# Folding the memory's weights outside the mixers of a two-layer hybrid encoder

## Chip, cores, metric

One NeuronCore of a Trainium2 chip runs the whole program; nothing is shared with other cores. The metric is device time of one execution in microseconds, and lower is better.

## What is computed

The trunk has two layers over 1024 tokens of width 1024, in float32. Each layer projects its input into four mixers (axial GQA attention, bidirectional RWKV-7, bidirectional HGRN2, MLA attention), joins them, adds a cross-attention to 256 memory tokens and then a mixture of 32 experts:

```python
for l in range(DEPTH):
    h = x @ w_in[l]
    z_att, z_rwkv, z_hgrn, z_mla = split_sizes(h, (ATT_IN, RWKV_IN, HGRN_IN, MLA_IN))
    ...
    mix = jnp.concatenate([y_att, y_rwkv, y_hgrn, y_mla], axis=-1) @ w_out[l]
    x = layer_norm(DN_ALPHA * x + mix, ln1_g[l], ln1_b[l])
    x = layer_norm(DN_ALPHA * x + memory_cross_attention(x, mem, mem_wq[l], mem_wkv[l], mem_wo[l]),
                   ln2_g[l], ln2_b[l])
    x = layer_norm(DN_ALPHA * x + hierarchical_moe(x, ...), ln3_g[l], ln3_b[l])

def memory_cross_attention(x, mem, wq, wkv, wo):
    q = (x @ wq).reshape(B, S, MEM_HEADS, dh)
    k, v = jnp.split(mem @ wkv, 2, axis=-1)
    ...
    return block_attention(q, k, v, dh ** -0.5) @ wo
```

The memory `mem` is an input of the program, so the products `wq @ k^T` and `v @ wo` of each head don't depend on the tokens. The kernel computes them once per layer ("the fold") and then multiplies the tokens with the folded 1024 x 1024 matrices `wqk` and `vw`.

## The kernel before

Every large product is done in three passes: a float32 operand is split into a high part (ScalarE copies it into the fp32r type) and the remainder (VectorE subtracts), and TensorE multiplies high by high, high by low and low by high into one PSUM bank (`mm3`, L256 to L260). So each weight of 128 x 2048 costs a load of 1 MB, a ScalarE copy and a VectorE subtraction before its last pass can run.

A layer has these stages, in program order (a scheduler then orders each engine's queue from it):

- `in_proj` (L338): eight tiles of 128 tokens come from a generator (`ln_in` for layer 0, the `combine` of the experts' outputs for layer 1). Each is transposed, split and multiplied with the two weights `w_ina` (`values`, 272 columns, L258 to L260), then twenty weights `w_inb` follow (L719). All its raw weights go through the two buffers of the pool `k.raw`.
- The mixers (in `trunk`): `rwkv` runs woven with `beside()`, which first runs the two attentions and then `hgrn` woven with `mem_prep`, the fold. `weave` takes the next step from the generator that is furthest behind its share; the shares are `RW, SPLIT` (rwkv against the rest) and `SHARES` (hgrn against the fold). `SPLIT` 2.13 lets attention, which counts 1, run beside the first 1/2.13 of rwkv's steps.
- `mem_prep` (L1537): per head and layer a product of `mem_wkv` with the memory (twice, for keys and values: 96 matmuls of 256 columns in all), `wqt` with the keys (48 of 256) and the values with `wo` (24 of 512). Over four heads these are 576 matmuls of 256 columns and 96 of 512. Its weights come in pieces of 256 KB through two buffers `mz` (L1549), are split by L1550 (ScalarE) and L1551 (VectorE), and the results are copied out (L1582, L1595) and stored to HBM.
- `Weights` is the ring that loads (L1644) and splits (L1654, L1655) all later weights, up to 10 raw buffers and 4 split ones ahead; `mix_mem` and `moe` take them with `W.next()` and let the next one be split with `W.ahead()`.
- `moe` (L2028): 32 experts; the rows of an expert's output are scattered to HBM (L2078), and `combine` (L2147) loads them again (L2162), adds them (L2178), normalises (L285 to L295) and yields the tiles to the next `in_proj`. Its pools are opened on the right side of the memory, where the ring's buffers were.

## Time and profile before

| what | us |
|---|---|
| median of 3 runs | 3597.49 |
| lowest and highest of them | 3592.26, 3612.54 |
| the profiled execution | 3598.46 |
| its span | 3596.6 |

The profiled execution is 1 us from the median, and 1.9 us of it lie outside its span. In the profile a busy time of an engine is the union of its instructions' spans. Matmuls are pipelined, so that the distance between the starts of two of them is shorter than their duration. A window's row gives the busy time of each engine in a stretch of the span, and the share of full clock that was granted to TensorE there (1.00 is 2.4 GHz, 0.50 is 1.2 GHz).

### The profile page before, as it was taken

To read this page: it belongs to the slowest core of one execution; us is meant where nothing else is said; L and a number is where in the kernel's file an instruction comes from. 1 tells how busy PE (TensorE), PEld (TensorE's weight loads), DVE (VectorE), ACT (ScalarE), POOL (GpSimd) and SP (SyncE) were. 2 spreads that over 40 slices of the span, in tenths; PEclk is the share of its full clock that TensorE was granted. 3 is DMA by queue.
4 is the path that set the end of the run, shared out by engine and by line. 5 is a ranking of instruction groups with operands and counts; after the bars stand their busy time and mean duration, and the time that the engine had idled before them with its cause. 6 is when DMAs were issued, how large, how long until landed. Compare 5 with 4: busy or idle time off the path is not lost. (4 is left out here: it accounts for less than half of the span.)

```text
span 3596.6 us, 57124 instructions
## 1 busy us (share of the span) xinstructions
PE 3179.0 (88%) x22814; PEld 2394.0 (67%) x22814; DVE 2489.7 (69%) x3966; ACT 1577.5 (44%) x2303; POOL 745.1 (21%) x496
## 2 busy tenths in 40 slices
PE   8999799988969997999599888989888699979995
PEld 7867345557857886777487564454677588867772
DVE  6546877668846466899764578767788364669996
ACT  3344333345432222788534353433454323138883
POOL 0000353421020003332210004533200200033323
PEclk9999799899989997999799988988899899979997
DMA  5223411125464132999542252111344741249994
GB/s 212 109 74 134 99 34 46 42 75 152 122 216 157 61 135 108 342 363 372 210 160 109 81 158 43 52 28 45 97 146 119 255 158 59 88 155 362 365 341 186
DMA packets 270217, 545.74 MB, mean 152 GB/s; under 512 B 90608, under 2 KB 170096, under 8 KB 236400
## 3 DMA queue, kind: packets, MB, share of 16 engines
q1 hardware_dynamic: 244496, 486.31, 39.5%
q0 software_dynamic: 24288, 53.52, 4.2%
q8 instruction: 184, 3.01, 0.3%
q10 hardware_dynamic: 1152, 2.10, 0.2%
q14 instruction: 97, 0.79, 0.1%
HBM read 444.29 MB, written 131.07 MB: 160 GB/s over the span
## 5 line engine op out<-in xcount | busy, mean ns | idle before, releaser
L1655 DVE TENSOR_TENSOR wl<-raw,wh 128x2048 fp32r<-128x2048 f32 x202 | 465.2, 2306 | 69.5 <-ACT wh L1654 66.6
L1654 ACT ACTIVATE wh<-raw 128x2048 fp32r<-128x2048 f32 x216 | 413.4, 1914 | 161.8 <-PE y L260 102.4
L1432 POOL TENSOR_TENSOR acc<-acc,pT 128x512 f32<-128x512 f32 x224 | 312.4, 1418 | 326.5 <-PE o L1429 197.0
L258 PE MATMUL bg<-wh,xh 128*128 128x512 f32 x768 | 310.3, 404 | 45.6 <-ACT xh L1696 45.6
L260 PE MATMUL bg<-wh,xl 128*128 128x512 f32 x768 | 307.9, 401 | 5.0 <-DVE xl L1697 4.9
L259 PE MATMUL bg<-wl,xh 128*128 128x512 f32 x768 | 308.2, 401 | 0.0
L1410 DVE TENSOR_REDUCE nm<-c 128x1 f32<-128x512 f32 x236 | 161.8, 685 | 109.8 <-PE c L1409 107.6
L1443 ACT ACTIVATE pT<-b 128x512 f32<-128x512 f32 x224 | 128.1, 595 | 211.2 <-PE b L1441 198.4
L719 PE MATMUL p<-xh,wh 128*128 128x512 f32 x640 | 208.1, 404 | 0.9 <-DVE r L569 0.9
L258 PE MATMUL h<-wh,xh 128*128 128x512 f32 x512 | 207.9, 406 | 0.2 <-ACT xh L309 0.2
L309 ACT ACTIVATE xh<-tp 128x512 fp32r<-128x512 f32 x224 | 122.9, 599 | 185.1 <-PE tp L307 175.7
L260 PE MATMUL h<-wh,xl 128*128 128x512 f32 x512 | 202.5, 395 | 0.0
L259 PE MATMUL h<-wl,xh 128*128 128x512 f32 x512 | 202.3, 395 | 0.0
L719 PE MATMUL p<-xl,wh 128*128 128x512 f32 x640 | 200.3, 392 | 0.0
L719 PE MATMUL p<-xh,wl 128*128 128x512 f32 x640 | 199.4, 391 | 0.0
L258 PEld LDWEIGHTS bg<-wh,xh 128*128 128x128 f32 x768 | 146.6, 191 | 79.1 <-ACT xh L1696 47.2
L1655 POOL TENSOR_TENSOR wl<-raw,wh 128x2048 fp32r<-128x2048 f32 x14 | 63.7, 4565 | 632.3 <-ACT wh L1654 616.9
L958 POOL DMA_DIRECT2D xs<-zlo x48 | 26.5, 556 | 779.3 <-DVE raw L512 660.6
L2078 POOL DMA_INDIRECT ya<-yo,slot x64 | 93.3, 1458 | 403.9 <-DMA ya<-yo,slot 178.1
L260 PEld LDWEIGHTS bg<-wh,xl 128*128 128x128 f32 x768 | 146.2, 190 | 40.3 <-DVE xl L1697 7.9
L259 PEld LDWEIGHTS bg<-wl,xh 128*128 128x128 f32 x768 | 146.6, 191 | 32.1
L310 DVE TENSOR_TENSOR xl<-tp,xh 128x512 fp32r<-128x512 f32 x224 | 146.1, 682 | 29.4 <-ACT xh L309 23.1
(518 smaller groups left out, 8023.5 us busy)
## 6 DMA issues: line engine op xcount, KB each, us to landing
raw<-in_moe_w_dram SPq DMA_DIRECT2D x192, 1024.0 KB
raw<-in_w_inb_dram SPq DMA_DIRECT2D x20, 1024.0 KB
x<-x SPq DMA_DIRECT2D x40, 512.0 KB
mz<-in_mem_wkv_dram SPq DMA_DIRECT2D x64, 256.0 KB
mz<-in_mem_wqt_dram SPq DMA_DIRECT2D x32, 256.0 KB
wqk<-rec SPq DMA_DIRECT2D x32, 256.0 KB
mz<-in_mem_wo_dram SPq DMA_DIRECT2D x32, 256.0 KB
vw<-rec SPq DMA_DIRECT2D x32, 256.0 KB
```

Source lines behind the costliest of these rows:

```text
L258: self.T.matmul(ps, ah, bh, start=start, stop=False)
L259: self.T.matmul(ps, ah, bl, start=False, stop=False)
L260: self.T.matmul(ps, al, bh, start=False, stop=stop)
L309: self.S.activation(out=h, in_=p, func=AF.Copy)
L310: self.V.tensor_tensor(xl[:, 4 * j:4 * j + 4], p, h.bitcast(F32), ALU.subtract)
L719: T.matmul(p[i], a, b[i][:, kk], start=(kk == 0 and a is h and b is xh), stop=(kk == 7 and a is lo))
L1410: V.reduce_max(nm[:, j, t, c:c + 1], b, axis=AX.X)
L1432: G.tensor_tensor(acc[j], acc[j], p[j], ALU.add)
L1443: S.activation(out=p[j], in_=b, func=AF.Exp, scale=scale)
L1654: k.S.activation(out=h, in_=raw, func=AF.Copy)
L1655: (k.G if pool else k.V).tensor_tensor(lo, raw, h.bitcast(F32), ALU.subtract)
L2078: G.indirect_dma_start(out=y_d, out_offset=bass.IndirectOffsetOnAxis(ap=ai, axis=0), in_=y, in_offset=None, bounds_check=2047, oob_is_err= ...
```

## The change

The fold leaves the mixers. `mem_prep` becomes a generator that takes its weights, banks and staging buffers from its caller. Layer 0's runs inside `in_proj`: after each tile's transposes three of its 24 steps are issued, before the `values` of the tile ahead. Layer 1's runs at the end of layer 0's `moe`, behind the last expert's `down`, with its weights supplied by the same `Weights` ring; for this, three buffers of the ring (`W.late`) are lent to the memory tokens from expert 26 on. All weights of the fold now come as whole 1 MB loads. `ln_in` has two buffers where it had three, hgrn has four PSUM banks where it had two, and the shares in the weave are new: attention runs beside the first 1/1.5 of rwkv.

```diff
-RW, SPLIT, ATT, SHARES = 420, 2.13, 1 / 90, (70, 12)
+RW, SPLIT, ATT, HGRN = 420, 1.5, 1 / 90, 1 / 157
...
 def ln_in(k):
-        pl = k.pool(es, "lnin", 3, side="right")
+        pl = k.pool(es, "lnin", 2, side="right")
...
 def in_proj(k, l, src, fold):
+        def folding():
+                load = lambda dt=F32: k.t(k.raw, [128, 2176], "raw", dt)[:, :2048]
+                raw = load().rearrange("p (k n) -> p k n", k=8)
+                nc.sync.dma_start(raw, A["mem_t"])
+                mem = [k.t(pl, [128, 8, 256], t, F32R) for t in ("mh", "ml")]
+                k.split_into(raw, *mem)
...
+                def weight():
+                    raw = load()
+                    nc.sync.dma_start(raw, next(srcs))
+                    h, lo = k.t(pl, [128, 2048], "fh", F32R, bufs=2), load(F32R)
+                    k.split_into(raw, h, lo)
+                    return h, lo
...
         for t, x in src:
             k.transpose_split(x, xh[t // 4][:, :, o:o + 128], xl[t // 4][:, :, o:o + 128], pt)
+            for _ in islice(extra, 3):
+                pass
             if t:
                 values(t - 1)
+        for _ in extra:
+            pass
         values(7)
...
+def mem_prep(k, mem, weight, done, bank, wide, stage, halves, wqk, vw):
...
+    for hd in range(4):
+        kh, kl = mem_proj()
+        yield
+        wh, wl = weight()
+        for g in range(2):
+            b = wide()
...
+            dma(wqk[hd - hd % 2 + g, :, :, n], out(b).rearrange("p (m n) -> p m n", m=4))
             yield
...
+        vh, vl = mem_proj()
+        yield
+        wh, wl = weight()
+        for t in range(2):
+            b = wide()
...
 class Weights:
     def fetch(self, q=None):
+        if self.lent and self.wr[0] is self.late:
+            self.wr.popleft()
+            return
...
 def moe(k, l, x2_d, lg, sl, W, fold):
+            if e == 26 and fold:
+                W.lend()
+        ht, w2 = turn(pt, h), W.next()
+        down(py, ht, w2, aid[:, 31:32])
+        if fold:
+            W.ahead()
...
+            for _ in mem_prep(k, (mh, ml), W.next, W.ahead, lambda: k.t(ps, [128, 512], "h"), wide,
+                              lambda: k.t(pl, [128, 1024], "yo", bufs=NY), spare, *fold):
+                pass
...
 def trunk(nc, tc, A, out, nl=2, dbg=None):
-                        sh = k.pool(es3, "psh", 2, PSUM)
-                        sm = k.pool(es3, "psm", 2, PSUM)
-                        yield from weave([hgrn(k, Z, l, mix_d, cp, ph, sh, pe, first),
-                                          mem_prep(k, l, raw, wqk, vw, ph, pe, sm)], SHARES)
+                        sh = k.pool(es3, "psh", 4, PSUM)
+                        for c in hgrn(k, Z, l, mix_d, cp, ph, sh, pe, first):
+                            yield (c or SMALL) * HGRN
```

SyncE's queue at the program's start, where the first weights are loaded. Before:

```order
L365 DMA raw_159<-in_w_ina_dram 128x2176
L334 DMA xd_71<-y_76 128x1024
L365 DMA raw_165<-in_w_ina_dram 128x2176
L328 DMA x_191<-in_x_dram 128x1024
L328 DMA x_277<-in_x_dram 128x1024
L328 DMA x_363<-in_x_dram 128x1024
L365 DMA raw_869<-in_w_inb_dram 128x2048
L365 DMA raw_991<-in_w_inb_dram 128x2048
```

Now (`mem_t` is the memory, `mem_wkv` and `mem_wqt` are the fold's weights; all go through the two buffers of `k.raw`):

```order
L369 DMA raw_163<-in_w_ina_dram 128x2176
L338 DMA xd_71<-y_76 128x1024
L369 DMA raw_169<-in_w_ina_dram 128x2176
L332 DMA x_329<-in_x_dram 128x1024
L430 DMA raw_198<-in_mem_t_dram 128x2048
L332 DMA x_516<-in_x_dram 128x1024
L437 DMA raw_204<-in_mem_wkv_dram 128x2048
L332 DMA x_727<-in_x_dram 128x1024
L332 DMA x_914<-in_x_dram 128x1024
L437 DMA raw_263<-in_mem_wqt_dram 128x2048
L338 DMA xd_71<-y_331 128x1024
L338 DMA xd_71<-y_518 128x1024
```

The fold's loads follow the two of `w_ina` at once, and those of `w_inb` come behind the fold.

TensorE's queue in the same stage. Before, the values of tile 0 (`p<-w,x`) follow the first transposes:

```order
L307 MATMUL tp_177<-ident,y_76 128x128 x4
L307 MATMUL tp_184<-ident,y_76 128x128 x4
L258 MATMUL p_223<-wh_161,xh_138 128x272
L259 MATMUL p_223<-wl_162,xh_138 128x272
L260 MATMUL p_223<-wh_161,xl_140 128x272
```

Now, from the end of the third weight of the fold on (`fh` and `raw` are a weight's halves, `mh`, `ml` the memory's, `mph` those of a head's keys or values):

```order
L262 MATMUL p_367<-mh_200,fh_363 128x256
L263 MATMUL p_367<-ml_201,fh_363 128x256
L264 MATMUL p_367<-mh_200,raw_364 128x256
L311 MATMUL tp_745<-ident,y_729 128x128 x4
L311 MATMUL tp_752<-ident,y_729 128x128 x4
L311 MATMUL tp_932<-ident,y_916 128x128 x4
L262 MATMUL p_426<-fh_422,mph_416 128x512
L262 MATMUL p_427<-fh_422,mph_416 128x512
L262 MATMUL p_444<-fh_422,mph_416 128x512
L262 MATMUL p_445<-fh_422,mph_416 128x512
L262 MATMUL p_462<-wh_165,xh_142 128x272
L263 MATMUL p_462<-wl_166,xh_142 128x272
```

Three weights of the fold, 48 matmuls each, stand ahead of the first `values`; the later ones alternate with them.

VectorE's and GpSimd's queues between layer 0's experts and layer 1's projection. VectorE before:

```order
L2066 TENSOR_TENSOR htl_17566<-tp_17562,hth_17565 128x256
L383 TENSOR_TENSOR c_2969_17678<-ppt_119 128x8
L389 MEMSET tiny_17682 128x1
L393 TENSOR_TENSOR lbe_17685<-ppt_119 128x2
L384 TENSOR_SCALAR c_2969_17678<-c_2969_17678 128x8
L395 TENSOR_TENSOR lbe_17685<-ppt_119,lbe_17685 128x2 x2
L397 TENSOR_TENSOR lbe_17685<-lbe_17685 128x2
L398 RECIPROCAL lbe_17685<-lbe_17685 128x2
L399 TENSOR_TENSOR lb_17684<-lbe_17685 128x2
L400 TENSOR_SCALAR lb_17684<-lb_17684 128x2
L2178 SCALAR_TENSOR_TENSOR x_17607<-y_17613,gate_14427,x_17607 128x1024 x2
```

VectorE now (`wl` is the split of a fold's weight, `xg` the low half of a head's keys or values):

```order
L1690 TENSOR_TENSOR wl_17938<-raw_17566,wh_17937 128x2048
L1690 TENSOR_TENSOR wl_17991<-raw_17609,wh_17990 128x2048
L1589 TENSOR_TENSOR xg_18080<-h_18031,xg_18080 128x512
L1589 TENSOR_TENSOR xg_18190<-h_18141,xg_18190 128x512
L2235 SCALAR_TENSOR_TENSOR x_18247<-y_18253,gate_14181,x_18247 128x1024 x2
L289 BN_STATS st_18267<-x_18247 128x6 x2
```

GpSimd now (before, both `wl` stand ahead of the first `x`):

```order
L2113 DMA ya_14156<-yo_17374,slot_11704 2048x1024
L373 TENSOR_TENSOR wl_18337<-raw_18334,wh_18336 128x2176
L299 TENSOR_TENSOR x_18247<-x_18247,b_2969_18246 128x1024
L373 TENSOR_TENSOR wl_18343<-raw_18340,wh_18342 128x2176
L299 TENSOR_TENSOR x_18250<-x_18250,b_2969_18246 128x1024
```

The whole combine stays behind the fold on VectorE, and the splits of `w_ina` stand between its first tiles on GpSimd.

## Rows read from the trace of the kernel before

**Rows 1.** The page: the span, and each engine's busy time.

```profile
span 3596.6 us, 57124 instructions
...
PE 3179.0 (88%) x22814; PEld 2394.0 (67%) x22814; DVE 2489.7 (69%) x3966; ACT 1577.5 (44%) x2303; POOL 745.1 (21%) x496
```

**Rows 2.** Windows: attention's and hgrn's part of the mixers, both layers.

```profile
core 0: us, PE busy (x) PEld busy (x) DVE busy (x) ACT busy (x) POOL busy (x), PEclk, DMA share, GB/s
...
395.00:766.00 371.00, 340.58 (x2518) 179.01 (x2519) 269.45 (x441) 132.07 (x230) 169.50 (x128) 0.88 0.15 40
766.00:1045.00 279.00, 239.21 (x4108) 209.15 (x4108) 221.17 (x493) 136.86 (x242) 22.20 (x17) 0.96 0.46 139
...
2150.00:2538.00 388.00, 350.23 (x2649) 186.78 (x2648) 287.98 (x472) 144.73 (x251) 172.70 (x134) 0.89 0.17 44
2538.00:2832.00 294.00, 246.85 (x4111) 215.83 (x4109) 220.63 (x492) 138.66 (x245) 22.72 (x18) 0.93 0.45 137
```

**Rows 3.** Groups by line from 766 to 1045: the fold's, and hgrn's scan.

```profile
L1551 DVE TENSOR_TENSOR raw<-mz,raw 128x512 fp32r<-128x512 f32 x64 | 43.8, 696 | 20.8 <-ACT raw L1550 20.5
L1342 DVE SCALAR_TENSOR_TENSOR hx<-hx,dec,h 128x64 f32<-128x64 f32 x56 | 17.3, 309 | 1.1
...
L1566 DVE TENSOR_TENSOR mpl<-b,mph 128x256 fp32r<-128x256 f32 x16 | 6.7, 417 | 2.2 <-ACT mph L1565 2.1
```

**Rows 4.** The tile `mh`: its subtraction, both layers.

```profile
L1556 DVE TENSOR_TENSOR ml<-raw,mh x2: 2273/2273/2273, 774.5 to 2546.2; 128x2048 fp32r<-128x2048 f32 x2
```

**Rows 5.** Timeline: starts of the fold's matmuls at 784 and 791 us.

```profile
784.09 0.41 PE L258 MATMUL b<-mh,raw 128*128 128x256 f32 x1
784.30 0.41 PE L259 MATMUL b<-ml,raw 128*128 128x256 f32 x1
...
790.82 0.28 PE L258 MATMUL b<-mh,raw 128*128 128x256 f32 x1
790.93 0.28 PE L259 MATMUL b<-ml,raw 128*128 128x256 f32 x1
791.05 0.28 PE L260 MATMUL b<-mh,raw 128*128 128x256 f32 x1
```

**Rows 6.** Timeline, start of the program: one weight's way, and `values`.

```profile
8.03 0.33 SPq L365 DMA_DIRECT2D raw<-in_w_ina_dram  x1
...
13.12 2.02 ACT L368 ACTIVATE wh<-raw 128x2176 fp32r<-128x2176 f32 x1 [0.30 <-DMA raw<-in_w_ina_dram]
15.17 2.42 DVE L369 TENSOR_TENSOR wl<-raw,wh 128x2176 fp32r<-128x2176 f32 x1 [1.62 <-ACT wh L368]
...
19.21 2.43 DVE L369 TENSOR_TENSOR wl<-raw,wh 128x2176 fp32r<-128x2176 f32 x1
...
25.04 0.29 PE L258 MATMUL p<-wh,xh 128*128 128x272 f32 x1
25.17 0.28 PE L259 MATMUL p<-wl,xh 128*128 128x272 f32 x1
```

**Rows 7.** Line L258 from 0 to 130 us: number, first and last start.

```profile
L258 PE MATMUL p<-wh,xh x128: 285/289/594, 15.2 to 79.1; 128*128 128x272 f32 x128
```

**Rows 8.** Timeline from layer 0's last expert to layer 1's first transpose.

```profile
1746.01 0.39 PE L259 MATMUL y<-wl,hth 128*128 128x512 f32 x1
1746.24 0.40 PE L260 MATMUL y<-wh,htl 128*128 128x512 f32 x1
...
1755.74 1.27 SPq L2162 DMA_DIRECT2D y<-ya  x3
...
1757.97 9.50 POOL L369 TENSOR_TENSOR wl<-raw,wh 128x2176 fp32r<-128x2176 f32 x2 [4.46 <-ACT wh L368]
...
1767.60 2.60 DVE L2178 SCALAR_TENSOR_TENSOR x<-y,gate,x 128x1024 f32<-128x1024 f32 x2
...
1785.18 1.97 PE L307 MATMUL tp<-ident,x 128*128 128x128 f32 x8 [38.55 <-POOL x L295]
```

**Rows 9.** Timeline behind layer 0's mixers: the ring's first split.

```profile
1047.70 3.94 ACT L1654 ACTIVATE wh<-raw 128x2048 fp32r<-128x2048 f32 x2 [0.88 <-DMA vw<-rec]
```

More of the change, by code (lines that the diff above doesn't have):

```diff
@@ L253, in split_sb, with split_into @@
         return h, l
+    def split_into(self, raw, h, l):
+        self.S.activation(out=h, in_=raw, func=AF.Copy)
+        self.V.tensor_tensor(l, raw, h.bitcast(F32), ALU.subtract)
     def mm3(self, ps, a, b, start, stop):
@@ L335, in ln_in, with in_proj @@
             yield t, y
-def in_proj(k, l, src):
+def in_proj(k, l, src, fold):
     nc, A, V, S, T = k.nc, k.A, k.V, k.S, k.T
@@ L419, in values @@
                 V.tensor_copy(kr[:, t, 16 * c:16 * c + 16], p[:, 256:272])
+        def folding():
+            with ExitStack() as es:
+                pl = k.pool(es, "mp", 1)
+                load = lambda dt=F32: k.t(k.raw, [128, 2176], "raw", dt)[:, :2048]
[3 more added lines that the diff above has]
+                k.split_into(raw, *mem)
+                srcs = mem_weights(A, l)
+                def weight():
[4 more added lines that the diff above has]
+                    return h, lo
+                bank = lambda: k.t(ps, [128, 512], "p")
+                yield from mem_prep(k, mem, weight, lambda: None, bank, lambda: (bank(), bank()),
+                                    lambda: k.t(pl, [128, 1024], "mo"),
+                                    lambda: [k.t(pl, [128, 512], t, F32R) for t in ("mph", "mpl")], *fold)
+        extra = folding() if fold else iter(())
         k.ln_exp()
@@ new lines, in mem_proj, with out @@
+                c = slice(256 * kk + 128 * e, 256 * kk + 128 * e + 128)
+                k.mm3(b[:, 256 * e:256 * e + 256], (wh[:, c], wl[:, c]), (mem[0][:, kk], mem[1][:, kk]),
+                      kk == 0, kk == 7)
+        done()
+        h, lo = halves()
+        S.activation(out=h, in_=b, func=AF.Copy)
+        V.tensor_tensor(lo, b, h.bitcast(F32), ALU.subtract)
+        return [a.rearrange("p (e n) -> p e n", e=2) for a in (h, lo)]
+    def out(b):
+        o = stage()
+        for i, x in enumerate(b):
+            S.activation(out=o[:, 512 * i:512 * i + 512], in_=x, func=AF.Copy)
+        return o
@@ L1601 @@
+            c, m = divmod(2 * hd + t, 4)
+            dma(vw.rearrange("(n c) p m w -> c m p n w", c=2)[c, m], out(b).rearrange("p (n w) -> p n w", n=2))
+            yield
+        done()
 class Weights:
@@ L1606, in __init__ @@
         self.k, self.es, self.srcs = k, es, iter(srcs)
-        self.raw, self.ready = deque(), deque()
+        self.raw, self.ready, self.lent = deque(), deque(), False
         self.wp = deque([k.pool(es, "ewr", 3, side="right")] * 3)
@@ L2033, in moe @@
         xp = k.pool(es, "ex", 1)
-        xg = [xp.tile([128, 1024], F32, name=k.uid("xg")) for _ in range(NX)]
+        xg = [k.t(xp, [128, 1024], "xg", bufs=NX) for _ in range(NX)]
         for x in xg:
@@ L2239, in trunk_consts, with weights @@
     k.lgp = k.pool(es, "lgp", 1)
-def weights(A, l, wqk, vw):
+def weights(A, l, wqk, vw, more):
     fl = lambda a: a.rearrange("p k n -> p (k n)")
@@ L2253, in weights @@
     yield fl(A["moe_w2"][l, 31])
+    if more:
+        yield from mem_weights(A, l + 1)
 def trunk(nc, tc, A, out, nl=2, dbg=None):
@@ L2262, in trunk @@
         ppt = [k.cload(f"ppt{l}", A["pp"][l], [128, NPP]) for l in range(2)]
+        fold = [[k.dt([4, 128, 4, 512], n) for n in ("wqk", "vw")] for _ in range(nl)]
         for l in range(nl):
+            wqk, vw = fold[l]
             def pp(n, i=None, t=ppt[l]):
```

101 lines of the change are left out of this document (38 added, 63 removed).

## The prediction

> **What bounds the kernel now.** I read the page first. TensorE is busy for 3179 of 3596.6 us, VectorE for 2490, ScalarE for 1578 [rows 1], so TensorE is where a moved product has to find room. But an average over stages doesn't say what the fold costs where it stands, so I went to windows [rows 2]. The mixers of layer 0 are two stretches. From 395 to 766 us attention runs beside rwkv: TensorE is busy for 341 of 371 us (92%), VectorE for 269 (73%), at a granted clock of 0.88. From 766 to 1045 hgrn, the rest of rwkv and the fold run together: TensorE 239 of 279 (86%), VectorE 221 (79%), at 0.96. Layer 1 has the same two stretches of 388 and 294 us. In neither is one engine full; three generators fill each other's waits in the second stretch, two in the first.
>
> Then the fold's own rows. On VectorE it holds 43.8 + 6.7 us of the second stretch [rows 3] and 2.3 for the memory's split [rows 4], 52.8 in all. On TensorE its matmuls of 256 columns start 0.12 us apart at full clock, and 0.21 at half clock after a pause [rows 5]; those of 512 columns start 0.23 us apart beside the experts [rows 8]. So a layer's fold is 576 x 0.12 + 96 x 0.23 = 69 + 22 = 91 us of TensorE that nothing can be laid over, since it uses the whole array.
>
> **Layer 0: the price beside the projection.** In the timeline a weight takes 5.1 us from its load's issue to ScalarE's copy, 2.0 for the copy and 2.4 for the subtraction [rows 6], 9.5 us. `k.raw` has two buffers. One holds a weight's low half until its matmuls are over, the other can take the next load only behind the subtraction, so the fold's weights follow each other at 9.5 us, while each has 5 to 6 us of matmuls. The first of them can be loaded when the second `w_ina` is split, at 21.6 us [rows 6], and is ready at 31.1. By the order of TensorE's queue three weights stand ahead of the first `values`, so nothing fills the gaps there: the fourth is ready at 59.6. TensorE then has 74 us of fold left, 384 matmuls of `values` at 0.13 us [rows 6], 50 us, and some 5 of transposes: it is done at 189 at the earliest. The chain of weights says nearly the same: 12 more at 9.5 us bring 174, and the last product and the `values` behind it 16 more. Two lanes of the same length don't cover each other fully, so I take 195. Today the last of these matmuls starts at 79.1 us [rows 7]. **Cost 116 us**, between 101 (TensorE never waits from 31 us on: 31 + 91 + 50 + 8) and 131 (1.3 us more per weight). The smaller `ln_in` pool and the fold's loads and stores on SyncE's queue, with the token tiles queued behind them, are priced at nothing: the 91 us of matmuls cover them, and where they don't, that is in the upper end.
>
> **Layer 1: the price behind the experts.** The ring supplies split weights four ahead, so TensorE is the limit: 91 us, and 4 for the first waits of a head's keys. The transition behind it gets shorter. Now TensorE stands for 38.5 us between its last expert and its first transpose [rows 8]: 9 until the outputs can be loaded (the last scatter), 12 until VectorE begins (GpSimd splits both `w_ina` for 9.5 of them), and 17.6 of combine. With the fold ahead of it the scatter is long over. Yet the combine itself doesn't move beneath the fold: its pools lie on the ring's memory, and VectorE's queue has it behind the fold's last split. GpSimd's queue now has a split of `w_ina` (half of 9.5) ahead of tile 0, and ScalarE's copy for it is late too. So 5 for a load, 17.6, and 4 for the split: 27 us, between 18 (loads and split hidden) and 38.5 (nothing gained). **Cost 95 + 27 - 38.5 = 83 us**, from 74 to 95.
>
> **What the mixers give back.** Two changes act there. Attention now runs beside 1/1.5 of rwkv's steps in place of 1/2.13: counted in the two orders, 414 of rwkv's 2176 rows on TensorE move ahead of attention's end, out of 1218 that stood behind it. The first stretch gets longer. On TensorE these small matmuls are some 20 us, on VectorE some 35 (a third of what is left of 221 without the fold's 53 and hgrn's, which I put at 65 around its scan of 17.3 [rows 3]; an estimate). TensorE is fuller there, so I take 25: 371 becomes 396, 388 becomes 413. In the second stretch VectorE keeps 221 - 53 - 35 = 133 us. Which fill may it reach? Two generators are left, as in the first stretch, where it is 73% (74% in layer 1): 133 / 0.73 = 183, and 133 / 0.74 = 179. The gain is 371 + 279 - 396 - 183 = **71 us** in layer 0 and 388 + 294 - 413 - 179 = **90 us** in layer 1. Ends: if TensorE sets the pace, it keeps 239 - 95 - 20 = 124 us at its old fill of 86%, 145 (layer 1: 157), and the first stretch grows by 22: gains of 112 and 115. If hgrn's chain of single steps sets it and VectorE is filled to 65%, 205 us: gains of 49 and 64.
>
> The ring's first split waits for the fold's last store now [rows 9], and its first loads for `k.raw`; both are free earlier. I take 3 us per layer, from 0 to 8.
>
> **Sum** against the profiled execution of 3598.46 us: + 116 + 83 - 71 - 90 - 6 = +32, so 3630.5; the median of the runs is 1 us lower. **I predict 3630 us, 0.9% slower.** The change moves 2 x 91 us of TensorE out of stretches that have idle time of their own on it into two that, behind their start, have none.
>
> **A page against the trace.** TensorE's busy time is 92% in the first stretch and 86% in the second, but its weight loads are busy for 179 of 371 (48%) and 209 of 279 us (75%) [rows 2]. The Trainium skill, "Trainium Kernel Development and Optimization" (Performance Expectations), says that matmul busy time is a poor measure since matmuls are pipelined, and that the busy share of LDWEIGHTS is the better one. By that, the second stretch is the one that TensorE limits and the first is not; rwkv's steps would be nearly free in the first, the fold's removal would be worth all its matmuls, and the sum would come out near 3564, which is the second rival. I don't follow it fully, since VectorE's 133 us remain whatever TensorE does.
>
> **Rivals.**
> 1. *The mixers give back still less.* hgrn is one chain of steps through VectorE, ScalarE and TensorE, and without the fold's dense blocks TensorE pauses more. The trace has the clock at 0.88 where small matmuls and waits alternate and at 0.96 where the fold runs [rows 2], and half clock after a pause [rows 5]. With the 65% above: 22 + 26 us less given back, 3678. (The Trainium skill, "TensorE: Matmul & The Clock Gate", HAM oscillation, has idle gaps of TensorE bring back the half clock; the trace agrees in [rows 5], and no run yet shows it for these mixers.) Against it: ScalarE, which waits for the fold's loads today, is freed.
> 2. *Faster: the fold is what blocks the mixers.* Its 48 matmuls in a row hold TensorE's queue for 6 us, 10 at half clock, with rwkv's and hgrn's short steps queued behind. Then the mixers shrink to TensorE's remainder: gains of 112 + 115 + 6 = 233 against costs of 199, 3564. It decides from the point where the two layers together give back over 199 us. For it: TensorE's 86% and the page's rule. Against it: VectorE would have to be filled to 133 / 145 = 92%.
> 3. *Even.* The fold covers itself better: 101 in layer 0 and a gap of 18 in layer 1 (cost 175) with the mixers' gain of 167: 3607.
>
> That the change doesn't do what it says I leave out: the orders show both folds where they are said to be.
>
> **Chances.** The forecast, from 3605 to 3660 by its own bounds, 0.42; rival 1, 0.17; rival 2, 0.18; rival 3, 0.23. About 0.5% (18 us) is what a measurement of this kernel can tell from no change, so under 3579.5 is faster and over 3615.5 slower. Rival 2 and a little of rival 3 are faster: 0.19. Most of rival 3 and the lower edge of the forecast are the same: 0.25. The rest is slower: 0.56. The range from 3560 to 3690 takes in the three rivals' times and leaves out the far sides of rivals 1 and 2, below 2 in 10 together. Faster and same hold 0.44, so the likeliest case's own range stands above.
>
> **What the next profile would show.** Right, if the last 272-column matmul starts near 195 us and gaps show between the first three weights of the fold; if TensorE stands for some 27 us behind the fold of layer 1; if the first stretch of the mixers is longer than 371 and the second, counted from the end of attention, near 180 with VectorE at about 73%. Wrong towards faster, if that second stretch is under 150 us; wrong towards slower, if it is over 200 at a clock below 0.9, or if the fold beside the projection ends past 210.

## The result: 3.1% slower, and the profile after

| | before | after |
|---|---|---|
| median of 4 runs each, us | 3594.88 | 3710.52 |
| lowest and highest | 3591.18, 3612.54 | 3698.31, 3721.43 |
| profiled execution, its span | 3598.46, 3596.6 | 3714.55, 3712.7 |

The ratio is 1.0311 (95% interval 1.0262 to 1.0359). The direction was forecast; the time lies 80 us over the forecast of 3630 and above the range's end of 3690. The page of the changed kernel answers [rows 1]:

```profile
span 3712.7 us, 56602 instructions
...
PE 3210.3 (86%) x22814; PEld 2429.0 (65%) x22814; DVE 2474.2 (67%) x3854; ACT 1563.6 (42%) x2189; POOL 752.3 (20%) x496
```

TensorE is 31 us busier with the same 22814 matmuls (its mean granted clock is 0.909, before 0.926), and idle for 85 us more. To see where, I cut both spans at the same events: attention's first matmul, attention's last reciprocal, the last matmul of rwkv or hgrn, the last routing matmul (`bg`), the last expert's last matmul. First the windows of the kernel before (stretch and its length, then each engine's busy time with its instructions in brackets, the granted clock, DMA share, GB/s):

```profile
0.00:365.80 365.80, 333.70 (x1582) 268.50 (x1583) 208.65 (x286) 143.11 (x201) 1.69 (x7) 0.98 0.38 132
365.80:770.20 404.40, 360.95 (x2662) 191.46 (x2662) 298.04 (x488) 147.65 (x253) 173.66 (x136) 0.87 0.20 52
770.20:1046.40 276.20, 239.76 (x4108) 209.57 (x4108) 217.08 (x486) 134.65 (x241) 22.20 (x17) 0.95 0.47 141
...
1414.70:1746.80 332.10, 314.09 (x1474) 250.19 (x1473) 281.64 (x262) 251.12 (x252) 110.91 (x64) 0.98 0.87 319
1746.80:2138.30 391.50, 331.83 (x1582) 266.44 (x1582) 236.53 (x311) 169.06 (x227) 32.88 (x14) 0.93 0.39 137
2138.30:2542.00 403.70, 356.93 (x2662) 190.07 (x2662) 298.12 (x488) 147.53 (x253) 173.78 (x136) 0.88 0.20 51
2542.00:2827.90 285.90, 246.52 (x4108) 215.73 (x4108) 216.73 (x486) 133.84 (x241) 22.44 (x17) 0.93 0.45 136
```

The same stages of the changed kernel:

```profile
0.00:491.90 491.90, 431.06 (x2254) 359.17 (x2255) 253.43 (x311) 195.81 (x258) 1.63 (x7) 0.97 0.44 151
491.90:936.60 444.70, 392.82 (x3467) 217.09 (x3468) 325.53 (x572) 158.43 (x277) 176.98 (x143) 0.87 0.21 53
936.60:1124.10 187.50, 127.53 (x2630) 112.17 (x2628) 139.24 (x321) 68.00 (x105) 31.80 (x16) 0.77 0.21 63
...
1483.80:1831.30 347.50, 321.15 (x1517) 257.31 (x1517) 290.34 (x266) 257.47 (x256) 115.12 (x64) 0.96 0.89 326
1831.30:2326.10 494.80, 432.58 (x2213) 356.93 (x2212) 271.08 (x332) 218.35 (x282) 36.40 (x14) 0.93 0.42 147
2326.10:2765.80 439.70, 387.18 (x3467) 214.54 (x3468) 326.40 (x572) 158.37 (x277) 177.34 (x143) 0.88 0.21 53
2765.80:2952.20 186.40, 126.94 (x2630) 111.47 (x2629) 141.45 (x321) 67.90 (x105) 31.56 (x16) 0.77 0.21 64
```

| stage | before | after | difference | forecast |
|---|---|---|---|---|
| start to layer 0's attention | 365.8 | 491.9 | +126.1 | +116 |
| layer 0, attention beside rwkv | 404.4 | 444.7 | +40.3 | +25 |
| layer 0, hgrn and the rest of rwkv | 276.2 | 187.5 | -88.7 | -96 |
| layer 0, to the end of routing | 368.3 | 359.7 | -8.6 | -3 |
| layer 0's experts | 332.1 | 347.5 | +15.4 | 0 |
| last expert to layer 1's attention | 391.5 | 494.8 | +103.3 | +83 |
| layer 1, attention beside rwkv | 403.7 | 439.7 | +36.0 | +25 |
| layer 1, hgrn and the rest of rwkv | 285.9 | 186.4 | -99.5 | -115 |
| layer 1, to the end of routing | 366.7 | 358.5 | -8.2 | -3 |
| layer 1's experts, output | 402.0 | 402.0 | 0 | 0 |
| sum | | | +116.1 | +32 |

The 84 us between the two sums lie in three places: 36 behind layer 0's experts and in them, 38 in the mixers with the routing behind them (17 and 21), 10 beside the projection. The windows also tell what kind of time it is. Beside the projection TensorE is busy for 97 us more (431.06 - 333.70) and idle for 29 us more; behind the experts it is busy for 101 us more and idle for 2.5 more. **In neither new place did TensorE's idle time shrink; on balance the fold filled none of it.** In the second stretches, 112 to 120 us of TensorE went away, and the stretches became only 89 and 100 us shorter.

**Beside the projection.** The gap at the start and the first and last matmuls, in the timeline and by line (L262 and its neighbours are `mm3` now; the last start of `p<-wh,xh` answers [rows 7]):

```profile
30.70 0.58 PE L262 MATMUL p<-mh,fh 128*128 128x256 f32 x1 [18.81 <-ACT fh L256]
```

```profile
L262 PE MATMUL p<-mh,fh x128: 279/282/582, 30.7 to 183.3; 128*128 128x256 f32 x128
...
L262 PE MATMUL p<-wh,xh x128: 283/289/428, 64.7 to 205.3; 128*128 128x272 f32 x128
```

```profile
L256 ACT ACTIVATE fh<-raw x16: 1909/1915/1918, 28.7 to 183.9; 128x2048 fp32r<-128x2048 f32 x16
```

The first product starts at 30.7 us (forecast 31.1), the sixteen copies follow each other at (183.9 - 28.7) / 15 = 10.3 us (forecast 9.5), and the last `values` matmul starts at 205.3 (forecast 195).

**The experts.** ScalarE's longest wait from 1785 to 1831 us, and in TensorE's timeline the idle time that it causes:

```profile
ACT raw L256 <- DMA raw<-in_mem_t_dram: 7.2, 1, 7.2
```

```profile
1806.59 0.69 PE L2098 MATMUL tp<-ident,hh 128*128 128x128 f32 x2 [7.56 <-DVE hh L2092]
```

ScalarE's copy of the memory tokens stands in its queue ahead of the activations of expert 30, though the program writes it behind the last expert. Its load, issued at 1784.91, takes 12 us in the weights' stream. Counted from the first `y<-wh,htl` of one expert to that of the next, two steps near the end take 19.0 and 10.8 us where the others, the first and the last apart, take 9.9 to 10.0.

**The transition.** VectorE in the timeline from the fold's end at 1929.5 us on, GpSimd there, and TensorE's waits up to 2025 us; they answer [rows 8]:

```profile
1929.04 2.61 DVE L2235 SCALAR_TENSOR_TENSOR x<-y,gate,x 128x1024 f32<-128x1024 f32 x2 [8.16 <-DMA y<-ya]
...
1937.52 4.78 DVE L298 TENSOR_TENSOR x<-x,g 128x1024 f32<-128x1024 f32 x1 [1.71 <-ACT x L297]
...
1944.71 5.89 DVE L2235 SCALAR_TENSOR_TENSOR x<-y,gate,x 128x1024 f32<-128x1024 f32 x1
...
2017.04 1.23 DVE L298 TENSOR_TENSOR x<-x,g 128x1024 f32<-128x1024 f32 x1
```

GpSimd's splits of `w_ina` beside these:

```profile
1936.44 4.78 POOL L373 TENSOR_TENSOR wl<-raw,wh 128x2176 fp32r<-128x2176 f32 x1 [97.50 <-DMA b<-in_ln_b_dram]
...
1944.73 4.79 POOL L373 TENSOR_TENSOR wl<-raw,wh 128x2176 fp32r<-128x2176 f32 x1
```

TensorE's waits:

```profile
PE tp L311 <- POOL x L299: 32.6, 6, 15.5
```

TensorE stands for only 15.5 us behind the fold, where I forecast 27. But then it waits for the later tiles too, 32.6 us in all. The windows from the first transpose to the last `values` matmul, before and now, show what is lost behind the first tile:

```profile
1785.20:1850.80 65.60, 59.74 (x449) 58.20 (x450) 48.05 (x96) 33.63 (x58) 17.76 (x7) 0.95 0.51 182
```

```profile
1945.00:2038.70 93.70, 68.07 (x449) 65.18 (x450) 61.89 (x112) 39.08 (x64) 25.03 (x8) 0.80 0.47 172
```

The combine's last instruction on VectorE before (the first is in [rows 8]):

```profile
1833.79 1.22 DVE L294 TENSOR_TENSOR x<-x,g 128x1024 f32<-128x1024 f32 x1 [1.31 <-ACT x L293]
```

The stretch behind the first transpose is 93.7 us where 65.6 were. TensorE is idle for 25.6 us of it where it was for 5.9, and the same matmuls keep it busy for 8 us more, at a granted clock of 0.80 for 0.95. From the fold's end to the last `values` matmul it is 2038.7 - 1929.5 = 109 us; before, from the last expert's matmul to the same one, 104 (1746.8 to 1850.8). On balance nothing of the transition went beneath the fold.

### The profile page after: what moved, and what is told of

Read it like the earlier page. It is cut to its first block, busy times and chain, and to the rows that moved or that the text cites. A ratio compares the mean times of both kernels' runs of the same rounds, so it can differ in the third digit from the quotient of the medians.

```text
span 3712.7 us, 56602 instructions
## 1 busy us (share of the span) xinstructions
PE 3210.3 (86%) x22814; PEld 2429.0 (65%) x22814; DVE 2474.2 (67%) x3854; ACT 1563.6 (42%) x2189; POOL 752.3 (20%) x496
## 5 line engine op out<-in xcount | busy, mean ns | idle before, releaser
L1690 DVE TENSOR_TENSOR wl<-raw,wh 128x2048 fp32r<-128x2048 f32 x218 | 500.4, 2298 | 123.0 <-ACT wh L1689 120.0
L1689 ACT ACTIVATE wh<-raw 128x2048 fp32r<-128x2048 f32 x232 | 443.5, 1914 | 188.0 <-PE y L264 118.0
L262 PE MATMUL bg<-wh,xh 128*128 128x512 f32 x768 | 308.6, 402 | 37.9 <-ACT xh L1731 37.9
L262 PE MATMUL h<-wh,xh 128*128 128x512 f32 x512 | 207.6, 406 | 0.1
L262 PEld LDWEIGHTS bg<-wh,xh 128*128 128x128 f32 x768 | 145.7, 190 | 70.7 <-ACT xh L1731 38.7
L1440 PE MATMUL c<-kh,qh 96*128 96x512 f32 (+1 forms) x236 | 129.7, 550 | 52.7 <-DVE nm L1441 43.7
## 6 DMA issues: line engine op xcount, KB each, us to landing
raw<-in_moe_w_dram SPq DMA_DIRECT2D x192, 1024.0 KB, 10.2
```

What stands on the lines that cost most here:

```text
L262: self.T.matmul(ps, ah, bh, start=start, stop=False)
L1440: T.matmul(b, q[:, 128 * t:128 * t + 128], kk[:, 512 * c:512 * c + 512], start=True, stop=True)
L1689: k.S.activation(out=h, in_=raw, func=AF.Copy)
L1690: (k.G if pool else k.V).tensor_tensor(lo, raw, h.bitcast(F32), ALU.subtract)
```

## The experiments

My theory after the comparison: the fold's price at its new places is TensorE's full time plus the waits that its chains bring, and the mixers give back less than they could since the new share puts more of rwkv beside attention, where it is dearer. The rivals: the prices are losses in details and can be mended (then the change is even); the low clock of the second stretch is what holds the mixers back (the prediction's first rival).

The changed kernel's own runs spread over 23 us, and a single edit moves little more than that; so where an edit has one run I read the stage that was edited. Stages spread too among the kernels that don't touch them: the stretch from the fold's end to the last `values` matmul of layer 1 takes 109 to 111.5 us, layer 0's last `values` matmul starts between 199.3 and 205.3, layer 0's experts take 340 to 347 us, and its attention stretch with the new share 434 to 446. A difference within these spreads shows nothing by itself.

**1. The load of the memory tokens earlier.**

```diff
+            if e == 29 and fold:
+                raw = k.t(W.late, [128, 2048], "raw").rearrange("p (k n) -> p k n", k=8)
+                dma(raw, A["mem_t"])
```

> The changed kernel, with the load of the memory tokens issued beside expert 29 and no longer behind the last expert; nothing else moves. Theory A: the last experts of layer 0 are late (19.0 and 10.8 us between the first y matmuls of experts 29 to 31 where 9.9 is the pace) because ScalarE's copy of the tokens waits 7.2 us for their load, with the experts' own activations queued behind it, and because the clock falls after the pause of 7.6 us. Then the pace comes back to 9.9 to 10.5 us, and the span is 13 to 16 us shorter than 3712.7. Theory B: the ring with three buffers fewer falls behind, and the copy waits only because TensorE does. Then the two steps stay at 19 and 11 us, and the span changes by under 4 us.

Inconclusive. The copy came forward with the load and still waited 5.4 us for it; the steps were 17.2 and 10.7 us, the experts 346.2. The whole run was 16 us faster (3698.07), but 11 of that in layer 0's attention stretch, which the edit doesn't touch. The total came out as forecast, for another reason: without the stages it would have passed as proof.

**2. The copy itself held back.**

```diff
+            one = k.t(k.small, [128, 1], "one")
+            V.tensor_scalar(one, h[:, 0:1], 0.0, 1.0, ALU.mult, ALU.add)
+            S.activation(out=mh, in_=raw, func=AF.Identity, scale=one)
```

> The changed kernel, with ScalarE's copy of the memory tokens tied to the last expert's transposed rows (it is scaled by a one that is worked out from them), so that it can't stand ahead of the last experts' activations; the load stays where it was. From the end of layer 0's routing matmuls to the last expert's last matmul the five changed kernels so far take 344 to 347.5 us, the kernel before 332, and all of the difference lies in the steps of experts 29 and 30 (15.6 to 19 and 10 to 10.8 us in place of 9.9 and 8.2). Theory A: it is this copy's wait for its load (5.4 us even where the load was issued with expert 29, and its place in the queue came forward with it). Then the steps are 9.9 to 10.5 us, the stretch is 333 to 336, and the fold's first product starts at most 3 us late. Theory B: the ring, three buffers short, or its loads are behind. Then it stays over 343.

All steps but the last took 10.0 us, as in the two later kernels with this edit (runs 11 and 12); the kernels without it have 13.5 to 19.0 in this place. So the copy's wait is the cause of the late step (theory A). But little came of it: the experts took 340.2 us, not 333 to 336, and experts and fold together 440.8 us, where the changed kernel takes 445.7 and the others with the early copy 437 to 446. TensorE now waits in the last expert's own short chain, and the last two steps, 8.2 and 4.4 us before the change, are 10.0 and 7.3; why, no run shows. TensorE's waits there:

```profile
PE y L264 <- DVE htl L2101: 3.0, 5, 1.6
PE y L262 <- ACT hth L2100: 2.3, 1, 2.3
```

**3 to 5. The share beside attention.**

```diff
-RW, SPLIT, ATT, HGRN = 420, 1.5, 1 / 90, 1 / 157
+RW, SPLIT, ATT, HGRN = 420, 2.13, 1 / 90, 1 / 69
```

> The changed kernel with the old share of rwkv beside attention (2.13, and hgrn's scaled so that both still end together). From attention's first matmul to the last reciprocal of attention the changed kernel takes 445 us in layer 0 and 440 in layer 1 (before: 404 in both), from there to the last matmul of rwkv or hgrn 171 and 170 (before, with the fold: 268 and 278). Theory A: rwkv's steps cost the same wherever they stand, since both stretches are limited by the same chains. Then the first stretch is 404 again, the second is 40 longer, about 210, and the span changes by under 8 us. Theory B: it is the new share that costs: attention's stretch was full and hgrn's has room once the fold is gone. Then the second stretch grows by no more than 20 us, to 190 at most, and the span is 30 to 50 us shorter.

> The changed kernel with attention beside the first 1/2.8 of rwkv (1/1.5 there, 1/2.13 before and in the run with the old share), hgrn scaled to end with rwkv. With 1/2.13 attention's stretch fell by 43 and 36 us to 401 and 404, and the rest grew by 27 and 32 to 215 and 218. Theory A: attention's stretch is now as long as attention alone makes it, and every rwkv step moved behind it lengthens the rest: first stretch 385 to 400, second 235 to 250, the mixers 5 to 20 us longer than with 1/2.13. Theory B: rwkv's steps are still dearer beside attention: the first stretch falls below 385, and the mixers are 5 or more us shorter than with 1/2.13.

> The changed kernel with the old share of rwkv beside attention once more, now timed against the kernel before. One look had it at 3673 us, 1.0214 times the kernel before of that look, its mixers up to the end of the routing matmuls 79 and 81 us shorter than before the change, where those of the changed kernels with the new share are 62 and 70 us shorter. If that holds, the ratio lies between 1.018 and 1.025 and so apart from the changed kernel's interval of 1.026 to 1.036. If the look was a lucky one within the changed kernel's own spread (3698 to 3721), the ratio is over 1.026.

Both stretches of layer 0, first with 1/2.13 (the timed run), then with 1/2.8:

```profile
489.00:893.60 404.60, 359.81 (x2662) 191.64 (x2664) 298.87 (x488) 145.73 (x252) 174.11 (x136) 0.87 0.21 54
893.60:1108.50 214.90, 158.16 (x3436) 138.63 (x3436) 166.54 (x405) 82.68 (x132) 37.45 (x23) 0.80 0.25 73
```

```profile
488.10:864.90 376.80, 341.07 (x2204) 169.05 (x2206) 261.40 (x406) 135.94 (x232) 167.31 (x129) 0.90 0.20 54
864.90:1111.40 246.50, 181.09 (x3896) 157.50 (x3894) 190.49 (x487) 93.87 (x152) 45.40 (x30) 0.83 0.24 70
```

Going from 1/1.5 to 1/2.13 saves 40 us in the first stretch and costs 27 in the second; from there to 1/2.8 it saves 28 and costs 32. With 1/2.13 the first stretch is 404.6 us, as before the change (404.4): its growth is the share's alone. Of the three shares the old one is the best for the mixers without the fold, too. With the routing behind them, the mixers give back 79 and 81 us with it in the first run (76 and 85 in the timed one), where the eight kernels with the new share give back 56 to 73 in layer 0 and 65 to 75 in layer 1 (57 and 72 in the changed kernel). Neither theory of the first run was right as written: the second stretch grew by 27 to 32 us, more than B allowed, but the sum fell. (Its 171 and 170 us end before the last transposes; by the cuts used here they are 187.5 and 186.4.) With 1/2.8 the second stretch is 246 and 253 us, at the end of theory A's span, the first 377 and 374, below it, and the two together are 4 and 10 us longer than with 1/2.13: longer, as A has it. Timed, the kernel with the old share stands at 3679.01 us, 1.0214 times the kernel before (1.0188 to 1.0240), apart from the changed kernel's 1.0262 to 1.0359.

**6 to 8. The transition.** The combine's loads on another queue; a warm TensorE; both, with the split of `w_ina` on VectorE.

```diff
-                dma(ys[-1], y3[t])
+                G.dma_start(ys[-1], y3[t])
...
+            for i in range(56):
+                T.matmul(p, m2[:, :128], l2[:, :512], start=i == 0, stop=i == 55)
...
-        wa = [wload(..., 2176, k.G if l else V) for c in range(2)]
+        wa = [wload(..., 2176, V) for c in range(2)]
```

> The changed kernel with the loads of the experts' outputs in the combine issued from GpSimd's queue and no longer from SyncE's. From the end of layer 1's fold (1929.5) to the last 272-column matmul of layer 1's projection the changed kernel takes some 95 us, where before the change 88 lay between the last expert and the same matmul. Theory A: these loads are late since they are queued on SyncE behind the fold's last stores and behind the stores of the tiles ahead. Then VectorE's first wait of 8.2 us for y and TensorE's waits of 32.6 us for the tiles shrink, and the stretch is 8 to 15 us shorter. Theory B: the stretch is some 71 us of VectorE work in a chain with ScalarE and GpSimd, and no load decides. Then it changes by under 4 us.

> The changed kernel with 56 added matmuls of 512 columns behind layer 1's fold, whose result nobody reads, so that TensorE doesn't stand for the 15.5 us ahead of layer 1's first transposes. The granted clock is 0.73 from the fold's end to the last 272-column matmul. Theory A: the half clock after that pause lengthens the projection's matmuls and by that the stretch. Then it is 6 to 12 us shorter. Theory B: the tiles come one by one from VectorE, and a faster TensorE only waits longer for the next. Then the stretch changes by under 4 us, and the clock falls again behind the first tile.

> The changed kernel with three edits to the transition at once: the combine's loads on GpSimd's queue and the dummy matmuls behind the fold, which alone brought 7.0 and 4.0 us there, and the split of layer 1's w_ina on VectorE in place of GpSimd (beside GpSimd's, two VectorE instructions of the combine take 4.78 and 5.89 us where 1.23 and 1.28 are usual). From the end of layer 1's fold to the start of the last 272-column matmul the changed kernels take 109 to 110 us; before the change 104 us lay between the last expert's matmul and the same one. Theory A: VectorE has 71 us of combine in a chain there, and what was lost is its waits (29 us in all). With the waits gone the stretch is 92 to 98 us, as predicted blind. Theory B: the three overlap, and the chain through VectorE, ScalarE and GpSimd for each tile sets the pace: no better than the loads alone, 100 to 104.

From the fold's end to the last `values` matmul: 102.7 us with the loads moved (7 less than the 109 to 110 of the others, just under theory A's 8 to 15), 105.7 with the filler (4 less, between its two theories), 97.1 with all three. (The first expectation's 95 and 88 us end some 15 us short of the last such matmul.) The windows of the changed kernel and of the third run:

```profile
1929.50:2038.70 109.20, 68.25 (x449) 65.36 (x450) 74.02 (x132) 48.02 (x74) 32.37 (x10) 0.77 0.51 185
```

```profile
1908.60:2005.70 97.10, 70.14 (x490) 65.21 (x489) 72.61 (x134) 47.66 (x74) 22.62 (x13) 0.89 0.57 212
```

VectorE has 73 to 74 us of work there in either; its idle time is 35 us in the changed kernel and 24 with the edits. Of the 12 us that the three save, 7 and 4 are those of the first two alone; if they add up, under 2 are left for the third. Theory A's span held, at its upper end, and theory B's did not; but the waits are not gone, as theory A had them, only a third of them.

**9, 10. The start.** Values of tile 0 first; the weights' low halves in a buffer of their own.

```diff
-            for _ in islice(extra, 3):
-                pass
             if t:
                 values(t - 1)
+                for _ in islice(extra, 3):
+                    pass
```

```diff
-                    h, lo = k.t(pl, [128, 2048], "fh", F32R, bufs=2), load(F32R)
+                    h, lo = k.t(pl, [128, 2048], "fh", F32R, bufs=2), k.t(pl, [128, 2048], "fl", F32R, bufs=1)
```

> The changed kernel with the values of tile 0 ahead of the first product of layer 0's fold, and each tile's three steps behind the values. In the changed kernel the last 272-column matmul starts at 204 to 206 us, TensorE does nothing from 20 to 30.9 us, and the copies of the fold's sixteen weights follow each other from 28.9 to 184 us at 10 us each. Theory A: TensorE is what limits the stretch behind its start, so work in the first gap shortens it: the last such matmul at 192 to 197, the span 8 to 13 us shorter. Theory B: the chain of weights through the two raw buffers limits it (10 us of load, copy, subtraction and matmuls for each), and what TensorE does in its gaps changes nothing: 202 to 208.

> The changed kernel with the low halves of layer 0's fold weights in a buffer of their own, so that both raw buffers can take loads; to make room the input's layer norm works in place with three buffers, and the fold's outputs are staged in a buffer that is used later. Theory A (TensorE limits the stretch): the last 272-column matmul moves by under 5 us, 200 to 206. Theory B (the chain of weights limits it): a weight then takes 7 to 8 us in place of 10, and the last such matmul starts at 185 to 193, TensorE's own work from 31 us on being 148 us long.

The last `values` matmul starts at 198.3 and at 200.0 us. In the thirteen kernels whose start is not edited it starts between 199.3 and 205.3, most often near 202. In the second run the weights come faster ((170.5 - 29.0) / 15 = 9.4 us each, for 10.3, not the 7 to 8 of theory B), and the end doesn't move beyond this spread: the chain of weights alone isn't the limit. In the first run the end is some 4 us earlier, between the spans of its two theories and little outside the spread; with everything mended (run 11) the same edit gave 194.9. So work in TensorE's first gap does shorten the stretch, by less than the 8 to 13 us expected. Two lanes of nearly the same length, as I had supposed, fit both runs; none that shortens both lanes was made.

**11, 12. What mending is worth, and the place alone.** All of the above mended (old share, experiment 2, the transition, the values first); and the same with layer 0's fold back in its mixers as before the change.

```diff
-            Z = in_proj(k, l, src, fold[0] if l == 0 else None)
+            Z = in_proj(k, l, src, None)
...
+                        if l == 0:
+                            sh = k.pool(es3, "psh", 2, PSUM)
+                            sm = k.pool(es3, "psm", 2, PSUM)
+                            yield from weave([hgrn(k, Z, l, mix_d, cp, ph, sh, pe, first),
+                                              mem_prep_mix(k, l, raw, wqk, vw, ph, pe, sm)], (70, 12))
+                            return
```

> Everything mended that the runs so far point to, with both folds still outside the mixers: the old share, the values of tile 0 ahead of layer 0's fold, the late copy of the memory tokens, and the three edits to the transition. Theory A: what is lost is the place: TensorE's 91 us a layer cost 110 to 120 us where they now stand, and the mixers give back 80 for them. Then the sum is 2 x 80 against some 118 and 105, and the kernel is 50 to 65 us slower than before: ratio 1.014 to 1.018. Theory B: the losses are in the details, and with them mended the change is even: ratio below 1.007.

> Only layer 1's fold is moved, behind layer 0's last expert, with the mended copy and transition; layer 0's is back in its mixers as before the change, and attention runs beside 1/2.13 of rwkv in both layers. Theory A (each place has its own price, and they add): layer 0 as before, layer 1 gives back 80 and pays 100 to 112 (of it 98 for the fold and the rest in the last experts and the transition): 20 to 32 us slower, ratio 1.006 to 1.009, and the run with everything mended lies 35 to 45 us above it. Theory B: behind the experts the fold is cheaper than in the mixers, once the transition is mended: ratio at or below 1.000, and this version beats both kernels.

| | median us | ratio to before (3601.38 in this set) | 95% interval |
|---|---|---|---|
| all mended | 3663.45 | 1.0174 | 1.0146 to 1.0203 |
| layer 1's fold alone moved | 3624.54 | 1.0072 | 1.0046 to 1.0098 |

Theory A, in both. By the stages, with everything mended: layer 0 pays 116 us at the start (481.8 - 365.8) and gets 79 back; layer 1 pays 8 in the experts and 94 behind them and gets 76 back. 116 + 102 - 79 - 76 = 63, and 3 in the tail; the spans differ by 66. Moving layer 0 back saves 39 us. With layer 1's fold alone moved, 7.5 us in the experts and 94 behind them stand against 82 given back. Of the versions that were run with a fold outside the mixers none beats the kernel before; the last is slower by less than 1%.

**13 to 16. Is it the clock?** The old share, hgrn with three banks; then with added matmuls at hgrn's steps that nobody reads.

```diff
+                            for i in range(4):
+                                k.T.matmul(z[:, 128 * i:128 * i + 128], k.ident_r, k.ident_r, start=True, stop=True)
...
+                            k.T.matmul(z, k.ident_r, w, start=True, stop=True)
```

> The control for the next run: the changed kernel with the old share (1/2.13), hgrn with three PSUM banks in place of four. With four the second stretch of the mixers, from attention's last reciprocal to the last matmul of rwkv or hgrn, takes 215 us in both layers, TensorE 158 of it at a granted clock of 0.80, VectorE 166 (77%). Both theories expect 213 to 220 at the same clock.

> The control with four matmuls of 128 columns added at each of hgrn's steps (identity by identity into a bank of their own, nobody reads them; some 476 a layer, at 0.06 us each at full clock 28 us of TensorE). Theory A (first rival of the prediction): the half clock holds the second stretch back, since without the fold TensorE pauses between short chains. Then the clock rises to 0.9 or more, and the stretch gets shorter in spite of the added work: 195 to 208. Theory B: VectorE's 166 us and the chains through it set the length, TensorE has 57 us of room. Then the clock rises and the stretch stays at 213 to 222. Theory C: TensorE's queue sets it, each added matmul stands ahead of a short step: 230 or more.

> The control with three banks, with one matmul of 512 columns added at each of hgrn's 164 steps a layer (into a bank of its own, nobody reads it): at 0.23 us each, as the experts' matmuls start, 38 us of TensorE a layer, in a second stretch of 215 to 217 us in which TensorE is busy for 160 at a granted clock of 0.80. The 656 matmuls of 128 columns of the run before took 0.145 us each of the stretch and left the clock at 0.77, so it told nothing of a full clock. Theory A (the prediction's first rival: the half clock holds the stretch back): the clock rises to 0.9 or more, as beside the fold (0.95), and the stretch is no longer than 217 in spite of the added work. Theory C (what TensorE's queue holds is the length, at whatever clock): the stretch grows by 25 to 45 us, to 240 or more. Theory B (VectorE's chain sets it): 213 to 222, with the clock where it was.

> The same at every second step of hgrn: 82 matmuls of 512 columns a layer, 19 us of TensorE. Theory A: the clock rises, and the stretch is 205 to 215. Theory C: it grows by 12 to 23 us, half of the run with all of them. Theory B: no change, 213 to 220.

Layer 0's second stretch in the control, with the narrow filler, and with the wide filler at every step and at every second one:

```profile
890.60:1108.00 217.40, 159.57 (x3436) 139.88 (x3436) 165.59 (x405) 82.79 (x132) 37.55 (x23) 0.80 0.24 72
```

```profile
897.00:1207.40 310.40, 273.20 (x4092) 249.19 (x4092) 169.95 (x405) 82.88 (x132) 36.40 (x23) 0.77 0.17 50
```

```profile
887.20:1109.50 222.30, 187.66 (x3600) 154.89 (x3600) 167.12 (x405) 82.41 (x132) 36.49 (x23) 0.91 0.24 70
```

```profile
890.50:1110.50 220.00, 176.37 (x3518) 149.49 (x3518) 165.46 (x405) 85.70 (x134) 37.66 (x23) 0.85 0.23 71
```

The control's 217 and 215 us are those of four banks: the banks are not what holds the stretch. The narrow filler was wrongly sized: 656 matmuls a layer and not 476, and each took 0.14 us of the stretch, not 0.06. Its 310 us lie in theory C's span, but it filled TensorE (273 of 310 us) and left the clock low, so it says nothing of a full clock. The wide filler raised the clock from 0.80 to 0.91, and the stretch did not get shorter: 5 and 9 us longer in the two layers, for 38 us of added work (3 and 8 for 19 us). The kernels with the old share and no filler have 215 to 217 in layer 0 and 215 to 222 in layer 1, so that the lengthening is hardly outside their spread. None of the theories fits it whole: VectorE's 166 us stand in all of these, TensorE has room for most of 38 us, and a higher clock doesn't pay for the rest. Whether a full clock without any filler would shorten the stretch is not shown; no kernel here can give it one. That the low clock is what the mixers lost is no longer likely.

## Why the prediction missed

- **Layer 1's price behind the experts, the largest miss (119 for 83).** The fold itself was sized well: 98 us from the last expert's matmul to its own last one, for 95. The failed step is "27 us, between 18 and 38.5" for the transition. I took the chain up to the first tile, let it shrink by 11.5 us, and took the seven tiles behind it to cost what they had. The first gap shrank by more, to 15.5 us; the rest grew from 65.6 to 93.7. Before, VectorE began late and was then busy for 63 of 70 us, waiting for no load: 67 us from the combine's first instruction (1767.60) to its last (1835.0). Now it begins at once and waits inside, 89 us (1929.04 to 2018.3) for the same work, and the fold hides none of it, as the order on its queue had shown me. Moving the loads, warming TensorE and moving the split took 12 us out again; what the rest of the waits is, no run separates. The second failed step is the join between the last experts and the fold, which I had at nothing but the 4 us for the waits of a head's keys: the memory tokens' copy in ScalarE's queue makes the experts 15 us late, and when it is held back, 8 us are left.
- **The first stretch of the mixers (40 and 36 for 25).** The failed step is "TensorE is fuller there, so I take 25". The stretch's fill didn't change: TensorE 89 and 88%, VectorE 74 and 73%. I had VectorE's fill at hand and used it for the second stretch only; with it, my own 35 us of VectorE would have been 35 / 0.73 = 48 us. The 35 was too much: 325.53 - 298.04 = 28 us of VectorE moved, and 28 / 0.73 = 38 lies between the 40 and 36 measured. The step from 1/2.13 to 1/1.5 costs more than it saves, 13 and 8 us with the fold gone.
- **The second stretch came out, in part by luck.** VectorE's 133 us at 73% were 139 at 74% (141 at 76% in layer 1), and the lengths 187.5 and 186.4 us for 183 and 179. Less of VectorE's work had moved than I took, and the fill was a little higher; with the old share it is 77%, so 73% is no constant of two generators, and that VectorE sets this length is not shown. (Layer 1's difference is short by 15 us; 8 of them are the cut, which gives the old stretch 286 us where the forecast's had 294.) The clock fell to 0.77, as the first rival had it, and the length still came out.
- **Layer 0's start (126 for 116; 120 to 126 in the other kernels with this start)** lies inside its own bounds of 101 to 131. A weight took 10.3 us for 9.5; with the values first and everything else mended, 481.8 - 365.8 = 116 was reached.
- **The ring's earlier start:** the stages up to the end of routing are 8 to 9 us shorter, for 3, just over its upper end of 8. That all of it is the ring's was not tested.
- **The rivals.** The second (3564) fell: it needed gains of 112 and 115 us, and even with the old share, where no step of rwkv moves, the mixers and the routing behind them gave back 76 and 85. Some 800 more of rwkv's matmuls made the first stretch 40 us longer, not 22. The Trainium skill, "Trainium Kernel Development and Optimization" (Performance Expectations), names the busy share of LDWEIGHTS, beside the share of peak arithmetic, as a good measure of how close a kernel is to roofline (its limit); this case's trace doesn't bear it out as a measure of room, at 47% of the first stretch before (191 of 404 us) and 49% after. The first rival had the right sign, but not the mechanism: against the forecast the first stretches lost 26 us, hgrn's 12 by their lengths, and a filler that brought the clock back did not shorten hgrn's.

The sign came from the last sentence of the sum, and it stands: the fold was moved out of stretches that had idle time for a part of it (with the old share TensorE's busy time in the second stretch fell by 82 and 88 us, its length by 61 and 71) into two in which it filled none.

## What to carry to other kernels

Before moving dense work out of a mixed stage, measure what it costs there, by taking the stage's length without it: here some 80 us (76 to 85 with the old share), for a fold that alone on TensorE takes 98, so a new place had to be cheaper than 80. A transition in which one engine is busy nearly throughout doesn't get shorter by hiding its start alone; count that engine's work, and its waits, in all of it. When an edit is judged by a single run, cut the span at the same events and read the edited stage, not the total, beside that stage's spread in the kernels that don't touch it.

## What was not expected of the hardware

- While GpSimd subtracts a 128 x 2176 weight (from 1936.44 and from 1944.73, 4.8 us each), VectorE's `x<-x,g` takes 4.78 us and its `x<-y,gate,x` 5.89, where 1.23 and 1.28 are usual; both end 1.1 us after GpSimd's. The Trainium skill, "SBUF — State Buffer" (SBUF: two separate sides), has VectorE and GpSimd share one port pair under an exclusive lock; these rows agree. With the split on VectorE, the stretch gained under 2 us, if the three edits add up: the price is about that of the split itself.
- A busier TensorE did not have the higher clock: with the narrow filler it was busy for 273 of 310 us at 0.77, with the wide one for 188 of 222 at 0.91.
- A load of 1 MB that takes 5.6 us elsewhere (the median of `w_inb`'s on the page, 10.2 for the experts' own) took 12 us in the experts' stream. The copy that waited for it held ScalarE for 7.2 us and TensorE for 7.6.
